# A hybrid convolution decoder block on one core: tiles of h and y moved by 160 bytes, other due times for h, norm and gate of mixer B, squares and taps shared by two engines, products taken from PSUM

## The chip, the core and the metric

The kernel runs on one core of a Trainium2 chip. Its engines are TensorE (PE; the loading of its stationary operand is shown apart as PEld), VectorE (DVE), ScalarE (ACT), GpSimd (POOL) and SyncE (SP, which issues nearly all DMAs here). The metric is the device time of one execution in microseconds; less is better. The kernel before takes 1806.1 us, the median of 3 runs (1805.6 to 1812.25).

## The reference

All arithmetic is float32; x is 256 tokens by 4096 channels. With D = 4096:

```
mod = silu(c) @ w_ada + b_ada            # 4096 -> 3 * 4096: shift, scale, gate
h   = rmsnorm(x, norm_g) * (1 + scale) + shift
P   = h @ w_in                           # 4096 -> 14336 columns: a_b a_c a_x a_z b_v b_g b_z, 2048 each
y_a = a_b * conv3(a_c * a_x) * silu(a_z)               # causal, depthwise
u   = conv31(b_v * sigmoid(b_g)) + conv_b_b            # causal, depthwise, 31 taps
y_b = silu(layernorm(u, ln_b_g, ln_b_b)) * silu(b_z)
x   = x + gate * (concat(y_a, y_b) @ w_out)            # 4096 -> 4096
out = rmsnorm(x, final_g)
```

## The kernel before

**Matrix products in three pieces.** A float32 weight tile `w_r` (128 channels x 2 x 512 columns, 512 KB) is split into a high half `w_h` (ScalarE, L215) and a low half `w_l` (VectorE, L216); h and y are split alike by `hi_part` (ScalarE, L248) and `lo_part` (VectorE, L251). `products` (L233) issues for each 128 channels k and each of the two token halves three matmuls: high x w_h (L242), high x w_l (L243), low x w_h (L244). The weights are the moving operand (512 columns), h or y the stationary one. One k of one column tile is a *unit*: 6 matmuls. A *step* is one weight tile, mostly two units (12 matmuls). w_in takes 28 column tiles x 32 k = 896 units, w_out 8 x 32 = 256: 1152 units, 6912 matmuls, 591 steps. The names w0 to w590 in the program count the steps.

**Blocks.** h needs shift and scale of its own channels, and these need 134 MB of w_ada, so w_in isn't walked column tile by column tile. `BLOCKS` cuts the 32 k into six blocks of 2, 4, 4, 6, 8 and 8; in each block all 28 column tiles are visited, partial sums being kept in `acc` tiles in SBUF and copied back to PSUM by `seed` (L593). At the start of a block its first column tile takes all new k one after the other, so pairs of new hT tiles (`hT24` holds k = 24, 25) are first used one step apart. In the last block `take` (L596) brings the finished sums out through ScalarE with the activation that the column tile wants (sigmoid for b_g, SiLU for a_z and b_z).

**What sets the order.** The program is recorded in the order in which Python runs, and each engine works through its instructions strictly in that order. `now` counts units. Every step first calls `next_w`, which records the load and the two splits of the weight tile two steps ahead:

```
        raw = raws.tile([P, KD, CT], F32, tag="r", name=f"w{i}_r")   # 4 buffers
        nc.sync.dma_start(raw[:, part], src[k // KD][:, part])
        ...                                                           # hi, lo: pool split, 3 buffers each
        nc.scalar.copy(hi[:, part], raw[:, part])
        nc.vector.tensor_tensor(out=lo[:, part], in0=raw[:, part], in1=hi[:, part].bitcast(F32), op=ALU.subtract)
```

then the pending `take`, then `seed` where the column tile ends, then `run_due`, which pops whatever `put(t, f)` has registered for t <= now, and then the step's matmuls. `w_h` of step s+2 uses the buffer that the matmuls of step s-1 read, so it waits for the end of step s-1. `run_due` also fills in the sums for shift, scale and gate (`ada_steps`, L261: a 1 MB row tile in one of 3 buffers, one VectorE pass of 2048 elements) where a model of VectorE's and the DMA's load leaves room or the sum falls due.

**h.** `h_steps` (L309) makes a pair of h tiles in five pieces: fetch (SP loads `xc` into a tile of pool `big`), by_token (VectorE), by_channel (two ScalarE instructions), high (ScalarE), low (VectorE). `H_LEAD` says how many units before its first use each is put; `H_DUE` how many before that use its sums fall due.

**Mixer A and B.** `silu_gate_A` (L411) multiplies the four accumulated tiles pairwise, transposes them by PE into `psA`, and applies the 3 taps. `glu_B` (L453) multiplies v by sigmoid(g), transposes into `psU`, keeps `uT`, and registers 30 taps (`conv_tap`, L490) for each of the four groups: four ScalarE multiplications into `pr` and one VectorE addition into `cv`. `norm_B` (L501) is the layer norm, `gate_B` (L567) transposes z into `psZ` (a pool of two PSUM buffers shared with the other transposes) and multiplies. y goes through `split_y`. The first half of w_out's k (y_A, sums `pa`) runs while mixer B ends; the second half (sums `pb`) follows.

**Where tiles lie.** Pools lie behind each other in SBUF. `split` (w_h, w_l) starts at byte 4096, `big` (acc, xc, hT, yT, pr, cv and others, 34 tiles of 4096 bytes) at byte 32096, which is 62 x 512 + 352. The last column tile of w_out keeps the first five of its eight weight steps (`HOLD = 5`) in tiles of `big` instead of `split`, works through token half 0, and then through token half 1.

Of the kernel before, what the change touches and what calls it, by code (L numbers as in the profile page):

```python
# [49 lines left out]

H_LEAD = (9, 6, 4, 2, 1)
H_DUE = 8
A_STEP = 3
CONV_END = 86
NORM_AT = 88
NORM_STEP = 2
# [15 lines left out]
def _segments():  # L72

    order = [16, 20, 17, 21, 18, 22, 19, 23]
    order += [e + i for i in range(4) for e in (4, 8, 0, 12)]
    order += [24, 25, 26, 27]
    segs, done = [], dict.fromkeys(order, 0)
    for b in range(len(BLOCKS)):
        for n, e in enumerate(order if (len(BLOCKS) - 1 - b) % 2 == 0 else order[::-1]):
            k0, k1 = done[e], sum(BLOCKS[:b + 1]) - (KD if n < EARLY.get(b, 0) else 0)  # L80
            if b == 0 and n < ALONE:
                k1 = 1
            done[e] = k1
# [24 lines left out]
def decoder_block(ctx: ExitStack, tc: tile.TileContext, x, c, w_mod, w_gate, w_in, w_out, xt, pk, final_g, out):  # L108
# [237 lines left out]
    sums = const.tile([P, NS, 8], F32, name="sums")  # L346
    table(AF.Silu)
    for q in range(4):
        ps = pst(f"cps{q}")
        for h in range(2):  # L350
            nc.tensor.matmul(ps[:, h], ones[:1], crow[q][:1, h * CT:(h + 1) * CT], start=True, stop=True)
        nc.scalar.activation(out=cB[:, q * 1024:(q + 1) * 1024], in_=ps, func=AF.Silu)
        for i in ((), (0, 1), (2, 3, 4), (5, 6, 7))[q]:
            nc.scalar.activation(out=xn[i], in_=xn[i], func=AF.Square, accum_out=sums[:, i % 2, i // 2:i // 2 + 1])
    table(AF.Sqrt)
# [21 lines left out]
    first_h[1][0]()  # L377
    first_mod[2]()
    next_w()
    first_mod[3]()  # L380
    for f, _ in first_h[2:]:
# [29 lines left out]
    def silu_gate_A(i):  # L411

        p, xa, q, z = (acc[e] for e in (4 + i, 8 + i, i, 12 + i))
        tiles, pss = {}, {}

        def gates():
            nc.vector.tensor_tensor(out=p, in0=p, in1=xa, op=ALU.mult)
            nc.vector.tensor_tensor(out=q, in0=q, in1=z, op=ALU.mult)

# [22 lines left out]
        t = now + 2  # L442
        put(t, gates, 2.3)
        for j in range(4):
            t += A_STEP
            put(t, lambda j=j: turn(j))
            put(t + 0.1, lambda j=j: tap(j))
            put(t + 2, lambda j=j: rest(j), 1.15)

# [3 lines left out]
    def glu_B(i):  # L453
        nonlocal conv_start
        v, g = acc[16 + i], acc[20 + i]
        pss = {}

        def gated():
            nc.vector.tensor_tensor(out=v, in0=v, in1=g, op=ALU.mult)

# [16 lines left out]

        put(now + 2, gated, 1.15)
        for h in range(2):
            put(now + 5, lambda h=h: turn(h))  # L480
            put(now + 5.1 + h, lambda h=h: keep(h))
        put(now + 8, tap)
        conv_start = conv_start or now + 10
        w = (conv_end - conv_start) / 4
        for sh in range(1, TAPS):
            t = max(now + 10, conv_start + i * w)
            t += (sh - 1) * (conv_start + (i + 1) * w - t) / (TAPS - 1)
            put(t, lambda sh=sh, t=t: conv_tap(i, sh, t))
# [107 lines left out]
    def take(e, k1, ps):  # L596

        if e not in acc:
            acc[e] = bigt(f"acc{e}")
        func = AF.Copy  # L600
        if k1 == KT:
            func = AF.Sigmoid if 20 <= e < 24 else AF.Silu if e >= 24 or 12 <= e < 16 else AF.Copy
        nc.scalar.activation(out=acc[e], in_=ps, func=func)  # L603
# [200 lines left out]
```

## Time and profile before

| | |
|---|---|
| median of 3 runs | 1806.1 us |
| the profiled execution | 1817.72 us, of it 1815.9 us from the first to the last instruction |
| PE busy | 1702.5 us, 94% |
| VectorE, ScalarE busy | 1383.5 us (76%), 1171.3 us (64%) |
| mean granted clock of PE | 0.972 |
| DMA | 524 MB through SP's queue, mean 290 GB/s |

The profiled execution is the one whose rows are shown below; its stages are cut at the first matmul of weight steps 0, 96, 368, 464, 512 and 544 and at the last matmul, that is at 0, 162, 706, 898, 994, 1058 and 1152 units. Matmuls are pipelined, so that a matmul's duration is longer than the distance between two starts; the distance is what counts.

### The profile page before, as it was taken

The numbers are of one execution on the slowest core, as the hardware profiler recorded it, in microseconds if no ns is written. First come the engines' busy times: TensorE is split into PE (matmuls) and PEld (weight loads), VectorE is DVE, ScalarE is ACT, GpSimd is POOL, SyncE is SP. The second block draws the span as 40 slices with busy tenths as digits, with TensorE's granted clock in tenths as the row PEclk, the third lists the DMA queues.
The fourth block names the chain that finished last, engine by engine and source line by source line (L and its number), as shares of the span: only waits on it lengthen the run. The fifth ranks groups of instructions, "written<-read, shape, count | busy, mean of one in ns | idle before, by whom it ended". The sixth has DMA issues, their size and how long they took to land. (4 is left out here: it accounts for less than half of the span.)

```text
span 1815.9 us, 20052 instructions
## 1 busy us (share of the span) xinstructions
PE 1702.5 (94%) x7069; PEld 1347.3 (74%) x7069; DVE 1383.5 (76%) x1329; ACT 1171.3 (64%) x1587; POOL 1.0 (0%) x8
## 2 busy tenths in 40 slices
PE   5989989999799998899999979999999999969997
PEld 2767868888688886688888857777777888748885
DVE  4877867888688887688888858888888977736556
ACT  5776657655465555455555548999999887534444
POOL 0000000000000000000000000000000000000000
PEclk9999989999899999899999989999999999979998
DMA  8998989999799999699999977666565766537775
GB/s 311 387 351 302 346 310 349 373 375 381 264 364 377 371 379 346 249 361 375 380 370 378 353 261 282 220 222 196 172 196 188 264 188 187 172 105 231 233 233 184
DMA packets 122284, 526.02 MB, mean 290 GB/s; under 512 B 13476, under 2 KB 13764, under 8 KB 97608
## 3 DMA queue, kind: packets, MB, share of 16 engines
q1 hardware_dynamic: 121992, 524.36, 80.4%
q8 instruction: 56, 0.92, 0.2%
q10 hardware_dynamic: 192, 0.39, 0.1%
q14 instruction: 44, 0.36, 0.1%
HBM read 520.48 MB, written 4.21 MB: 289 GB/s over the span
## 5 line engine op out<-in xcount | busy, mean ns | idle before, releaser
L216 DVE TENSOR_TENSOR w_l<-w_r,w_h 128x1024 fp32r<-128x1024 f32 (+1 forms) x591 | 705.5, 1196 | 388.1 <-ACT w_h L215 387.1
L215 ACT CAST w_h<-w_r 128x1024 fp32r<-128x1024 f32 (+1 forms) x591 | 606.0, 1026 | 599.1 <-PE ps L244 428.1
L244 PE MATMUL ps<-w_h,hT 128*128 128x512 f32 x1792 | 724.9, 405 | 43.3 <-DVE hT L251 43.3
L242 PE MATMUL ps<-w_h,hT 128*128 128x512 f32 x1792 | 725.8, 405 | 19.9 <-ACT hT L248 11.6
L243 PE MATMUL ps<-w_l,hT 128*128 128x512 f32 x1792 | 721.2, 402 | 0.5 <-DVE w_l L216 0.3
L244 PEld LDWEIGHTS ps<-w_h,hT 128*128 128x128 f32 x1792 | 345.2, 193 | 134.0 <-DVE hT L251 50.6
L242 PEld LDWEIGHTS ps<-w_h,hT 128*128 128x128 f32 x1792 | 345.5, 193 | 111.1 <-ACT hT L248 13.5
L243 PEld LDWEIGHTS ps<-w_l,hT 128*128 128x128 f32 x1792 | 344.8, 192 | 84.5 <-DVE w_l L216 1.8
L494 ACT ACTIVATE pr<-uT,pks 128x255 f32<-128x255 f32 (+14 forms) x480 | 198.6, 487 | 0.6 <-DVE cv L497 0.5
L603 ACT ACTIVATE acc<-ps 128x1024 f32<-128x1024 f32 x163 | 166.3, 1021 | 0.0
L269 DVE CUSTOM_DVE_ANT_0 mod<-mod,cB,pts 128x2048 f32<-128x2048 f32 x64 | 150.2, 2347 | 1.9 <-DMA mod<-in_w_mod 1.9
L269 DVE CUSTOM_DVE_ANT_0 mod<-mod,cB,pks 128x2048 f32<-128x2048 f32 x64 | 150.2, 2346 | 0.7 <-DMA mod<-in_w_mod 0.7
L497 DVE TENSOR_TENSOR cv<-cv,pr 128x1020 f32<-128x1020 f32 (+14 forms) x120 | 138.5, 1154 | 0.0
L593 ACT COPY ps<-acc 128x1024 f32<-128x1024 f32 x135 | 136.4, 1010 | 0.0
L242 PE MATMUL pb<-w_h,yT 128*128 128x512 f32 x256 | 104.3, 407 | 0.0
L243 PE MATMUL pb<-w_l,yT 128*128 128x512 f32 x256 | 103.6, 405 | 0.0
L244 PE MATMUL pb<-w_h,yT 128*128 128x512 f32 x256 | 103.4, 404 | 0.0
L242 PE MATMUL pa<-w_h,yT 128*128 128x512 f32 x256 | 102.6, 401 | 0.0
L243 PE MATMUL pa<-w_l,yT 128*128 128x512 f32 x256 | 101.9, 398 | 0.0
L244 PE MATMUL pa<-w_h,yT 128*128 128x512 f32 x256 | 101.9, 398 | 0.0
L269 DVE CUSTOM_DVE_ANT_0 gate<-gate,cB,pts 128x2048 f32<-128x2048 f32 x32 | 75.1, 2346 | 0.0
L269 DVE CUSTOM_DVE_ANT_0 gate<-gate,cB,pks 128x2048 f32<-128x2048 f32 x32 | 75.1, 2346 | 0.0
(111 smaller groups left out, 655.3 us busy)
## 6 DMA issues: line engine op xcount, KB each, us to landing
w_r<-in_w_in SPq DMA_DIRECT2D x433, 512.0 KB, 5.5
mod<-in_w_mod SPq DMA_DIRECT2D x128, 1024.0 KB, 7.7
gate<-in_w_gate SPq DMA_DIRECT2D x64, 1024.0 KB, 7.5
w_r<-in_w_out SPq DMA_DIRECT2D x128, 512.0 KB, 4.1
w_r<-in_w_in SPq DMA_DIRECT2D x30, 256.0 KB, 3.9
xn<-in_x SPq DMA_DIRECT2D x8, 512.0 KB, 6.3
xr<-in_x SPq DMA_DIRECT2D x8, 512.0 KB, 6.4
out<-o SPq DMA_DIRECT2D x16, 256.0 KB, 2.5
```

Source lines behind the costliest of these rows:

```text
L215: nc.scalar.copy(hi[:, part], raw[:, part])
L216: nc.vector.tensor_tensor(out=lo[:, part], in0=raw[:, part], in1=hi[:, part].bitcast(F32), op=ALU.subtract)
L242: nc.tensor.matmul(out, ah, hi[:, i], start=f, stop=False, skip_group_check=seeded)
L243: nc.tensor.matmul(out, ah, lo[:, i], start=False, stop=False, skip_group_check=seeded)
L244: nc.tensor.matmul(out, al, hi[:, i], start=False, stop=l, skip_group_check=seeded)
L269: nc.vector.tensor_tensor_reduce(out=raw, in0=raw, in1=cB[:, q * ROW:(q + 1) * ROW], scale=1.0, scalar=pt if q else bias, op0=ALU.mult, op ...
L494: nc.scalar.activation(out=pr[:, j, sh:], in_=u[:, j, :S - sh], func=AF.Copy, scale=cbw[:, 4 * i + j, TAPS - 1 - sh:TAPS - sh])
L497: nc.vector.tensor_tensor(out=o[:, :, sh:], in0=o[:, :, sh:], in1=pr[:, :, sh:], op=ALU.add)
L593: nc.scalar.copy(ps, acc[e])
L603: nc.scalar.activation(out=acc[e], in_=ps, func=func)
```

## The change

Seven groups of edits:

- A tile of 40 floats (160 bytes) is added to pool `const`, so that `big` starts at byte 32256 = 63 x 512; `split` stays at 4096.
- `H_LEAD` and `H_DUE` put every piece of h earlier, `low` 3 units instead of 1 before the first use.
- The column order is changed so that g comes before v, and a_b last of its four; `take` then multiplies the second factor straight out of PSUM on VectorE, in place of a ScalarE copy and a later VectorE product.
- Steps of mixer A are 4 units apart instead of 3, its first transposes come 2 units after the last sum instead of 5; those of `glu_B` 2 and 4 units after instead of 5.
- Every third tap of the 31-tap convolution is four VectorE instructions (multiply and add) and none on ScalarE.
- The taps end, and the norm starts, 12 units earlier; the gate of mixer B takes 4 units per group instead of 2.
- At the start four of the eight sums of squares go to VectorE, and the fourth sum for channel 0 precedes the first weight tiles.

```
+FILL = 40
-H_LEAD = (9, 6, 4, 2, 1)
-H_DUE = 8
-A_STEP = 3
-CONV_END = 86
-NORM_AT = 88
+H_LEAD = (15, 9, 7, 5, 3)
+H_DUE = 10
+A_STEP = 4
+CONV_END = 74
+NORM_AT = 76
...
-    order = [16, 20, 17, 21, 18, 22, 19, 23]
-    order += [e + i for i in range(4) for e in (4, 8, 0, 12)]
+    order = [20, 16, 21, 17, 22, 18, 23, 19]
+    order += [e + i for i in range(4) for e in (4, 8, 12, 0)]
...
+    const.tile([P, FILL], F32, name="fill")
...
+        if i % 2 == 0:
+            nc.scalar.activation(out=xn[i], in_=xn[i], func=AF.Square, accum_out=total)
+        else:
+            nc.vector.tensor_tensor_reduce(out=xn[i], in0=xn[i], in1=xn[i], ..., accum_out=total)
...
-        for i in ((), (0, 1), (2, 3, 4), (5, 6, 7))[q]:
+        for i in ((1, 2, 3), (4, 5), (6, 7), ())[q]:
...
+    first_mod[3]()
     next_w()
-    first_mod[3]()
...
-        put(t, gates, 2.3)
         for j in range(4):
-            t += A_STEP
-            put(t, lambda j=j: turn(j))
+            put(t + A_STEP * j, lambda j=j: turn(j))
...
-        put(now + 2, gated, 1.15)
         for h in range(2):
-            put(now + 5, lambda h=h: turn(h))
+            put(now + 2 + 2 * h, lambda h=h: turn(h))
...
     def conv_tap(i, sh, at):
         u, o = uT[i], cv[i]
+        if sh % 3 == 0:
+            for j in range(4):
+                nc.vector.scalar_tensor_tensor(out=o[:, j, sh:], in0=u[:, j, :S - sh], scalar=cbw[...], in1=o[:, j, sh:], op0=ALU.mult, op1=ALU.add)
+            return
...
+        other = {8: (e - 4, e - 4), 0: (e + 12, e), 16: (e + 4, e)}.get(e // 4 * 4)
+        if k1 == KT and other:
+            a, dst = (acc[j] for j in other)
+            nc.vector.tensor_tensor(out=dst, in0=ps, in1=a, op=ALU.mult)
...
-            t = end_in + NORM_AT + NORM_STEP * (18 + i + 0.5 * h)
+            t = end_in + NORM_AT + NORM_STEP * (18 + 2 * i + h)
...
-        put(t + 2.5, hi)
-        put(t + 3.5, lo, 0.65)
+        put(t + 2, hi)
+        put(t + 4, lo, 0.65)
```

VectorE's instructions around the first use of hT24 and hT26, at the start of the last block. PE reads hT24 in the step of w351, hT26 in that of w352. Before:

```order
L216 TENSOR_TENSOR w351_l_7347<-w351_r_7344,w351_h_7346 128x1024
L319 TENSOR_TENSOR xc26_7329<-xc26_7329,rstd_171 128x512
L269 ISA gate21_0_7355,pts_102<-gate21_0_7355,cB_103,pks_60 128x2048
L269 ISA pts_102 128x1
L216 TENSOR_TENSOR w352_l_7373<-w352_r_7370,w352_h_7372 128x1024
L319 TENSOR_TENSOR xc28_7350<-xc28_7350,rstd_171 128x512
L216 TENSOR_TENSOR w353_l_7398<-w353_r_7395,w353_h_7397 128x1024
L251 TENSOR_TENSOR hT24_7378<-xc24_7306,hT24_7378 128x2x256
```

After, in the same place:

```order
L218 TENSOR_TENSOR w351_l_7355<-w351_r_7352,w351_h_7354 128x1024
L321 TENSOR_TENSOR xc28_7292<-xc28_7292,rstd_172 128x512
L271 ISA gate21_0_7363,pts_103<-gate21_0_7363,cB_104,pks_60 128x2048
L271 ISA pts_103 128x1
L218 TENSOR_TENSOR w352_l_7381<-w352_r_7378,w352_h_7380 128x1024
L253 TENSOR_TENSOR hT24_7358<-xc24_7247,hT24_7358 128x2x256
L321 TENSOR_TENSOR xc30_7314<-xc30_7314,rstd_172 128x512
L218 TENSOR_TENSOR w353_l_7405<-w353_r_7402,w353_h_7404 128x1024
L253 TENSOR_TENSOR hT26_7385<-xc26_7267,hT26_7385 128x2x256
```

The low half of hT24 stood behind the split of w353 and stands now behind that of w352, one step earlier; a sum for gate (L271) stands ahead of that split.

SP's DMA issues at the same block start. xc28 goes into the tile that hT16 held, which PE reads last in the step of w347; xc30 into that of hT18, read last in the step of w348. Before:

```order
L210 DMA w350_r_7323<-in_w_in 128x1024
L316 DMA xc26_7329<-in_xt 128x512
L210 DMA w351_r_7344<-in_w_in 128x1024
L316 DMA xc28_7350<-in_xt 128x512
L268 DMA gate21_0_7355<-in_w_gate 128x2048
L210 DMA w352_r_7370<-in_w_in 128x1024
L316 DMA xc30_7376<-in_xt 128x512
L210 DMA w353_r_7395<-in_w_in 128x1024
```

After:

```order
L318 DMA xc26_7267<-in_xt 128x512
L270 DMA gate20_0_7269<-in_w_gate 128x2048
L212 DMA w348_r_7284<-in_w_in 128x1024
L318 DMA xc28_7292<-in_xt 128x512
L212 DMA w349_r_7306<-in_w_in 128x1024
L318 DMA xc30_7314<-in_xt 128x512
L270 DMA gate20_1_7316<-in_w_gate 128x2048
L212 DMA w350_r_7331<-in_w_in 128x1024
```

xc28, which waits for PE to end its work on hT16 (step of w347), stood ahead of the load of w352 and stands now ahead of that of w349; xc30 now ahead of that of w350.

VectorE's instructions for the gate of mixer B, its first three groups (`psZ1_0` is group 1, half 0). Before:

```order
L578 TENSOR_TENSOR cv0_7673<-cv0_7673,psZ0_0_11750 128x512
L216 TENSOR_TENSOR w529_l_11804<-w529_r_11801,w529_h_11803 128x1024
L578 TENSOR_TENSOR cv0_7673<-cv0_7673,psZ0_1_11777 128x512
L251 TENSOR_TENSOR yT8_11783<-cv0_7673,yT8_11783 128x2x256
L578 TENSOR_TENSOR cv1_7884<-cv1_7884,psZ1_0_11784 128x512
L216 TENSOR_TENSOR w530_l_11847<-w530_r_11844,w530_h_11846 128x1024
```

After:

```order
L584 TENSOR_TENSOR cv0_7651<-cv0_7651,psZ0_0_11549 128x512
L218 TENSOR_TENSOR w523_l_11599<-w523_r_11596,w523_h_11598 128x1024
L584 TENSOR_TENSOR cv0_7651<-cv0_7651,psZ0_1_11578 128x512
L253 TENSOR_TENSOR yT8_11577<-cv0_7651,yT8_11577 128x2x256
L218 TENSOR_TENSOR w524_l_11632<-w524_r_11629,w524_h_11631 128x1024
L584 TENSOR_TENSOR cv1_7865<-cv1_7865,psZ1_0_11608 128x512
```

Two half groups per step became one, and the whole has moved six steps ahead (w529 to w523).

## Rows read from the trace of the kernel before

**Rows 1.** Stages: us; PE, PEld, DVE, ACT, POOL busy; PE clock; DMA share, GB/s.
```profile
36.40:294.20 257.80, 241.89 (x972) 187.69 (x973) 196.45 (x196) 175.27 (x200) 0.00 (x0) 0.97 0.89 335
294.20:1113.60 819.40, 786.50 (x3273) 628.24 (x3272) 645.77 (x586) 456.46 (x481) 0.00 (x0) 0.97 0.93 349
1113.60:1413.40 299.80, 286.12 (x1242) 227.06 (x1241) 261.90 (x267) 284.36 (x514) 0.00 (x0) 0.99 0.63 204
1413.40:1549.70 136.30, 136.01 (x582) 109.14 (x581) 110.28 (x97) 111.34 (x201) 0.00 (x0) 1.00 0.68 211
1549.70:1671.30 121.60, 104.81 (x422) 83.13 (x421) 68.36 (x69) 58.84 (x75) 0.00 (x0) 0.90 0.52 163
1671.30:1802.90 131.60, 131.60 (x565) 106.00 (x563) 82.58 (x80) 62.38 (x81) 0.00 (x0) 1.00 0.68 222
```
**Rows 2.** The same view, of short stretches in which PE never waits.
```profile
80.00:100.00 20.00, 20.00 (x87) 16.10 (x86) 18.70 (x18) 13.37 (x16) 0.00 (x0) 1.00 1.02 414
440.00:460.00 20.00, 20.00 (x87) 16.09 (x86) 17.24 (x17) 13.45 (x16) 0.00 (x0) 1.00 1.02 406
900.00:1000.00 100.00, 100.00 (x428) 80.42 (x427) 82.22 (x71) 53.15 (x54) 0.00 (x0) 1.00 1.00 375
```
**Rows 3.** Timeline of PE, last token half: start, duration (us), engine, line, tiles, operands.
```profile
1793.39 0.39 PE L242 MATMUL pb<-w_h,yT 128*128 128x512 f32 x1
...
1798.83 0.40 PE L242 MATMUL pb<-w_h,yT 128*128 128x512 f32 x1
...
1799.53 0.39 PE L242 MATMUL pb<-w_h,yT 128*128 128x512 f32 x1
...
1802.34 0.40 PE L242 MATMUL pb<-w_h,yT 128*128 128x512 f32 x1
```
**Rows 4.** Waits (us, times, longest): stage one; stage two; whole span.
```profile
PE ps L244 <- DVE hT L251: 10.5, 5, 3.1
...
PE ps L244 <- DVE hT L251: 32.9, 11, 4.8
...
PE psZ L575 <- DVE cv L578: 16.5, 5, 3.7
```
**Rows 5.** Timeline of all engines at one start of a block (idle time before, releaser).
```profile
1055.68 1.04 ACT L215 CAST w_h<-w_r 128x1024 fp32r<-128x1024 f32 x1 [4.53 <-PE ps L244]
...
1056.76 1.23 DVE L216 TENSOR_TENSOR w_l<-w_r,w_h 128x1024 fp32r<-128x1024 f32 x1 [2.38 <-ACT w_h L215]
...
1057.90 0.69 DVE L251 TENSOR_TENSOR hT<-xc,hT 128x512 fp32r<-128x512 f32 x1
...
1058.64 0.79 PE L244 MATMUL ps<-w_h,hT 128*128 128x512 f32 x1 [2.52 <-DVE hT L251]
```
**Rows 6.** DMA issues: tile, queue, count, KB each, median us from issue to landing.
```profile
w_r<-in_w_out SPq DMA_DIRECT2D x128, 512.0 KB, 4.1
```
**Rows 7.** Timeline of all engines, start of the program.
```profile
3.18 13.99 PE L351 MATMUL cps<-crow,ones 1*128 1x512 f32 x16 [3.18 <-DMA crow<-in_c]
...
21.98 0.16 DVE L361 TENSOR_REDUCE tiny<-sums 128x2 f32<-128x8 f32 x1 [21.98 <-ACT xn L354]
...
31.13 1.89 DVE L216 TENSOR_TENSOR w_l<-w_r,w_h 128x512 fp32r<-128x512 f32 x3
...
32.93 2.35 DVE L269 CUSTOM_DVE_ANT_0 mod<-mod,cB,pts 128x2048 f32<-128x2048 f32 x1
...
36.41 0.79 PE L242 MATMUL ps<-w_h,hT 128*128 128x512 f32 x1 [9.20 <-ACT hT L248]
```
**Rows 8.** Groups by line: count, busy us, mean ns of one, idle before.
```profile
L494 ACT ACTIVATE pr<-uT,pks 128x255 f32<-128x255 f32 (+14 forms) x480 | 198.6, 487 | 0.6 <-DVE cv L497 0.5
L497 DVE TENSOR_TENSOR cv<-cv,pr 128x1020 f32<-128x1020 f32 (+14 forms) x120 | 138.5, 1154 | 0.0
L435 DVE SCALAR_TENSOR_TENSOR yfA<-psA,pks,yfA 128x255 f32<-128x255 f32 (+1 forms) x32 | 15.3, 480 | 0.9 <-ACT yfA L430 0.3
L673 DVE TENSOR_TENSOR o<-pb,gate 128x1024 f32<-128x1024 f32 x7 | 8.5, 1218 | 0.0
```

More of the change, by code (lines that the diff above doesn't have):

```diff
@@ L347, in decoder_block, with row_squares @@
     table(AF.Silu)
+    def row_squares(i):
+        total = sums[:, i % 2, i // 2:i // 2 + 1]
+        if i % 2 == 0:
+            nc.scalar.activation(out=xn[i], in_=xn[i], func=AF.Square, accum_out=total)
+        else:
+            nc.vector.tensor_tensor_reduce(out=xn[i], in0=xn[i], in1=xn[i], scale=1.0, scalar=0.0, op0=ALU.mult, op1=ALU.add, accum_out=total)
+    row_squares(0)
     for q in range(4):
@@ L352, in decoder_block @@
         nc.scalar.activation(out=cB[:, q * 1024:(q + 1) * 1024], in_=ps, func=AF.Silu)
-        for i in ((), (0, 1), (2, 3, 4), (5, 6, 7))[q]:
-            nc.scalar.activation(out=xn[i], in_=xn[i], func=AF.Square, accum_out=sums[:, i % 2, i // 2:i // 2 + 1])
+        for i in ((1, 2, 3), (4, 5), (6, 7), ())[q]:
+            row_squares(i)
     table(AF.Sqrt)
@@ L411, in silu_gate_A @@
     def silu_gate_A(i):
-        p, xa, q, z = (acc[e] for e in (4 + i, 8 + i, i, 12 + i))
+        p, q = acc[4 + i], acc[i]
         tiles, pss = {}, {}
-        def gates():
-            nc.vector.tensor_tensor(out=p, in0=p, in1=xa, op=ALU.mult)
-            nc.vector.tensor_tensor(out=q, in0=q, in1=z, op=ALU.mult)
         def turn(j):
@@ L442, in silu_gate_A @@
         t = now + 2
-        put(t, gates, 2.3)
         for j in range(4):
-            t += A_STEP
-            put(t, lambda j=j: turn(j))
-            put(t + 0.1, lambda j=j: tap(j))
-            put(t + 2, lambda j=j: rest(j), 1.15)
+            put(t + A_STEP * j, lambda j=j: turn(j))
+            put(t + A_STEP * j + 0.1, lambda j=j: tap(j))
+            put(t + A_STEP * j + 2, lambda j=j: rest(j), 1.15)
     uT, cv, zB = {}, {}, {}
@@ L454, in glu_B @@
         nonlocal conv_start
-        v, g = acc[16 + i], acc[20 + i]
+        v = acc[16 + i]
         pss = {}
-        def gated():
-            nc.vector.tensor_tensor(out=v, in0=v, in1=g, op=ALU.mult)
         def turn(h):
@@ L599, in take @@
             acc[e] = bigt(f"acc{e}")
[L600 to L603, printed above, removed]
+        other = {8: (e - 4, e - 4), 0: (e + 12, e), 16: (e + 4, e)}.get(e // 4 * 4)
+        if k1 == KT and other:
+            a, dst = (acc[j] for j in other)
+            nc.vector.tensor_tensor(out=dst, in0=ps, in1=a, op=ALU.mult)
+        else:
+            func = AF.Copy
+            if k1 == KT:
+                func = AF.Sigmoid if 20 <= e < 24 else AF.Silu if e >= 24 or 12 <= e < 16 else AF.Copy
+            nc.scalar.activation(out=acc[e], in_=ps, func=func)
         if k1 < KT:
             return
-        if 20 <= e < 24:
-            glu_B(e - 20)
+        if 16 <= e < 20:
+            glu_B(e - 16)
         elif e >= 24:
             zB[e - 24] = acc[e]
-        elif 12 <= e < 16:
-            silu_gate_A(e - 12)
+        elif e < 4:
+            silu_gate_A(e)
     def begin_step():
```

11 lines of the change are left out of this document (6 added, 5 removed).

## The prediction

> **What bounds the kernel now.** I read the table of stages first [rows 1]. PE is busy in 242 of 258 us, 786 of 819, 286 of 300, 136 of 136, 105 of 122 and 132 of 132, so PE is what the time is made of. How far is it from its own pace? Where it never waits it starts 428 matmuls in 100 us [rows 2], 233.6 ns each and 1.402 us per unit of 6. The six stages hold 162, 544, 192, 96, 64 and 94 units, which at this pace take 227.1, 762.7, 269.2, 134.6, 89.7 and 131.8 us; the stages lose 30.7, 56.7, 30.6, 1.7, 31.9 and 0 us over that. Before the first matmul lie 36.4 us [rows 7], after the last one 13.0. So 1,615 us are matmuls at pace, 152 us losses, 49 us ends.
>
> Then the waits [rows 4]: PE waited for the low half of hT 10.5 us in the first stage and 32.9 us in the second, and 16.5 us for the gate of mixer B. The rest of the losses in those stages is clock: a mean of 0.97 over 819 us means some 6% of it at the lower level (1.2 GHz), which costs half of that time, 25 us; 0.90 over 122 us costs 12 us. Each drop follows a wait. In the stage of 300 us there is little of either: ScalarE is busy in 284 of it, so there ScalarE is as much the bound as PE.
>
> **1. The 160 bytes.** Nearly all matmuls read weights at multiples of 4096 and hT or yT 352 bytes past a multiple of 512. The last column tile has both kinds side by side: five kept weight steps lie in the same pool as yT, three don't. In token half 1, 24 starts over kept tiles lie in 1793.39 to 1798.83, 226.7 ns each; 12 over the others in 1799.53 to 1802.34, 234.2 ns each [rows 3]. Same clock, same yT pool, no waits. I read this as: a matmul runs 6.8 ns faster where both operands start at the same place within 512 bytes (the kept tiles are all over the pool, so it is not one address). After the change all of them do. Per unit that is 41 ns, 1.402 to 1.361 us. I take it in full where PE sets its own pace: 544 units 22.2 us, 96 units 3.9, 64 units 2.6, 94 less the 10 kept ones 3.4; half of 6.6 us in the first stage, where DMA is at 414 GB/s [rows 2] and can't follow a faster PE; nothing in the 300 us stage (see 4). Sum 35.4. Can DMA follow elsewhere? At 375 GB/s and 1.402 us per unit [rows 2] it moves 0.526 MB per unit; at 1.361 us that is 386 GB/s, and 406 were reached with PE at full pace. Bounds: no gain at all if something other than the place within 512 bytes makes the difference; from below nothing excludes a loss, since no pair that starts at multiples of 512 on both sides is in the trace.
> A rule of the Trainium skill speaks against this edit: SBUF — State Buffer, section Door 1, says that SBUF is read in lines of 16 bytes and only crossing to a new line costs. Both 0 and 352 are line starts, so by it the edit is worth nothing and the sum would be 1716. The trace's 226.7 against 234.2 ns does not agree with it; it is the first rival.
>
> **2. h earlier.** What ends last at a block start is a chain [rows 5]: PE ends a step, w_h starts (1055.68), w_l follows (1056.76), and the low half of hT stands behind it (1057.90 to 1058.59): 2.9 us from release to end. It was recorded in the very step that needs it, so PE stops for 2.52 us, at each pair, and the clock falls. Recorded one step earlier, the same chain has 12 matmuls and the two that don't need the low half, 14 x 226.7 ns = 3.17 us: it fits, by 0.26 us. What is late next: in each of the last three block starts one sum of 2.35 us stands between (first excerpt): VectorE then is about 1.3 us late once or twice, 5 us in all. And the fetches, also earlier, now stand ahead of urgent weights (second excerpt): SP waits at xc28 until PE has left hT16, and queued behind it is w349, needed one step later. Issue to landing 4.1 us [rows 6], w_h 1.04 and w_l 1.14 make 6.3 us, less the 2.72 us step and one matmul: 3.3 us of stall; 2 more at w350; another 3.3 at the start two blocks' lengths before (xc22 before w238). Slow clock after these: some 4 us. So of the 56.7 us I leave 18 and take 38.7. In the first stage the low-half waits make 10.5 us; with a little of the clock I take 12.7 of the 30.7 lost, and leave 18 for slow first matmuls, late DMA and the earlier due times. Together 51.4; bounds 35 (every earlier piece late by a sum) and 70.
>
> **3. The start.** ScalarE's eight squares hold up the reduction until 21.98 [rows 7]. With four on VectorE, ScalarE is through when the last broadcast of c is (PE ends it at 17.2), and the root comes about 3.7 us earlier. The fourth sum (32.93) stood behind three weight splits (31.13, together 1.89 us); these now come after it, and only 0.63 us of them is in the way of the second matmul. 5.5 us; bounds 0 (its row tile lands late) and 6.
>
> **4. Mixer stage, 300 us.** 28 of some 84 taps in it move. Each takes four ScalarE instructions off (487 ns, 1.6 us overlapped) and one addition off VectorE (1.15), and puts four multiply-adds on it [rows 8]. The trace has these only from PSUM, in pairs that wait on each other: 480 ns. I bound one between 0.40 us (overlapping the next by 0.09, as w_l of 1.23 us is followed after 1.14 us in rows 5) and 0.515 (the 480 ns and a gap to the next, if each waits for the one before). So ScalarE goes from 284 to about 226 us, 12 copies of about 1 us gone too (w_h, as long, takes 1.04 in rows 5), and VectorE from 262 [rows 1] to between 275 and 288; I take 281. The products cost VectorE the same from PSUM as from SBUF (1218 ns for 1024 columns [rows 8]). PE itself needs 192 x 1.361 = 261 plus about 10 of transposes. So VectorE becomes the bound. Before, the stage took 5% over its busiest engine; I give VectorE 10 us for that: 291, a gain of 9; bounds 276 and 304.
>
> **5. Norm and gate of B.** Two half groups of psZ per step with two buffers made PE wait for VectorE's product, which stood behind a w_l that itself waited for PE: 16.5 us [rows 4] and 12 us of clock. Now one half group is done per step (third excerpt), and its product ends 2.9 us after a step's end by the chain of rows 5, as the buffer is wanted 2.72 us plus the transposes later: no wait. Transposes stay (31.9 - 16.5 - 12 = 3.4 us for 8 groups), and I leave 4 for the chain of the norm. Gain 24.4; bounds 10 and 28. The taps' earlier end costs nothing by itself: the stage behind has VectorE busy in 110 of 136 us.
>
> **Sum.** 35.4 + 51.4 + 5.5 + 9 + 24.4 = 125.7 us off the profiled span of 1815.9, giving 1690.2. The profiled execution took 1817.72 us (1.8 outside the span), 11.6 above the median of the runs; the runs differ in their stalls, and taking the same 125.7 off the median 1806.1 gives 1680.4. I forecast 1680.
>
> **Rivals.**
> - *The alignment does nothing*: 1680 + 35.4 = 1716. For it: kept and other tiles differ also in pool, and the two pools now agree within 512 but not within 1024 bytes. Against it: kept tiles at quite different addresses all run alike.
> - *It does more*: kept tiles and yT both lie 32 bytes past a multiple of 64, which may itself cost what the mismatch costs, 6.8 ns. Without it 219.9 ns, another 35 us: 1645. DMA would need 398 GB/s, under the 406 seen. The Trainium skill (TensorE: Matmul & The Clock Gate, back-to-back issue gap) gives about 216 ns for 512 columns at full clock; no row here comes near it, and by it the sum would be some 20 us lower still.
> - *VectorE is a harder bound than I think*: multiply-adds at 0.515 us, and its lag delays w_l in the stage behind too. 304 for 291, and 12 us more: 1705. For it: VectorE would be at 95% and works strictly in order.
> - *Slower than before*: the opposite of 1. If operands that both start at multiples of 512 bytes get in each other's way, every matmul pays: 6.9 us per ns. The other terms give 90 us, so it decides from 13 ns on, an interval of 247 ns; at 250 the time is 1829. For it: no row has such a pair. Against it: the kept pair agrees within 512 bytes too and is the faster one.
>
> **How the numbers follow.** Chances: forecast 0.62 (its own range 1655 to 1705), alignment nothing 0.20, more 0.10, VectorE 0.04, slower 0.04. The range that leaves out no more than 2 in 10 runs from 1640, which takes in the third case, to 1722, which takes in the first rival with some bad luck in 2 and 4. A difference of under 0.5%, 9 us, is what a measurement of this kernel can't tell from none. All cases but the last are faster by far more: faster 0.95, same 0.01, slower 0.04.
>
> **What would show it.** Step 1: starts 226.7 ns apart, some 441 matmuls per 100 us where PE doesn't wait; 428 would mean that the first rival holds. Step 2: the wait of PE for hT under 10 us instead of 43.4, clock at 0.99; new ScalarE waits for w_r's DMA of about 3 us at w238 and w349. Step 3: first matmul at 31 instead of 36.4. Step 4: VectorE over 95% busy in the mixer stage, w_h no longer waiting for ScalarE's taps. Step 5: no wait of psZ over 1 us. The forecast is wrong above all if the matmul interval is another, or if the new place of the fetches stalls PE for more than 10 us in all.

## The result, and the profile after

The changed kernel takes 1732.7 us, the median of 4 runs (1730.1 to 1740.1), against 1808.2 us (4 runs, 1805.6 to 1812.3): a ratio of 0.959 (0.955 to 0.963). It is faster by 4.1%, as its sign was forecast, but by 75 us where 126 were forecast, and the time lies above the range. The profiled execution took 1730.07 us with a span of 1728.3.

The stages of the changed kernel, cut at the same weight steps as [rows 1], with the same columns (the last window ends 1.1 us after the last matmul has started; the table behind it goes from start to start):

```profile
31.50:271.60 240.10, 230.26 (x972) 182.95 (x973) 197.63 (x198) 175.66 (x201) 0.00 (x0) 0.99 0.96 362
271.60:1043.60 772.00, 751.18 (x3276) 616.46 (x3275) 648.86 (x592) 459.11 (x487) 0.00 (x0) 0.99 0.96 372
1043.60:1348.20 304.60, 282.79 (x1239) 226.53 (x1238) 275.92 (x351) 233.79 (x393) 0.00 (x0) 0.98 0.62 199
1348.20:1480.20 132.00, 131.62 (x581) 108.75 (x580) 116.63 (x133) 92.37 (x145) 0.00 (x0) 1.00 0.68 216
1480.20:1587.80 107.60, 96.51 (x423) 77.70 (x422) 61.83 (x64) 55.31 (x72) 0.00 (x0) 0.97 0.60 187
1587.80:1716.60 128.80, 128.07 (x566) 105.70 (x564) 83.25 (x81) 62.53 (x81) 0.00 (x0) 1.00 0.70 229
```

Laid against the forecast stage by stage (the forecast is the length before, less the terms that the prediction gives to the stage):

| stage (units) | before | forecast | after | missed by |
|---|---|---|---|---|
| up to the first matmul | 36.4 | 30.9 | 31.6 | 0.7 |
| first (162) | 257.8 | 241.8 | 240.1 | -1.8 |
| second (544) | 819.4 | 758.5 | 772.0 | 13.5 |
| mixer (192) | 299.7 | 290.7 | 304.5 | 13.8 |
| w_out, y_A (96) | 136.3 | 132.4 | 132.1 | -0.3 |
| gate of B (64) | 121.6 | 94.6 | 107.6 | 13.0 |
| last (94) | 131.5 | 128.1 | 127.6 | -0.5 |

So three stages miss by 13 to 14 us each, and all else came out. The remaining 14 us of the miss are no stage's: the prediction took its 125.7 us off the median of three runs, which lay 11.6 us below the profiled execution that the terms were read from, and the profiled execution after lies 2.7 us below its own median.

The density of matmuls where PE never waits, against the last row of [rows 2]:

```profile
850.00:950.00 100.00, 100.00 (x443) 82.81 (x442) 85.48 (x73) 55.52 (x55) 0.00 (x0) 1.00 1.00 387
```

443 starts in 100 us instead of 428, and DMA follows with 387 GB/s (386 were worked out). The waits of the whole span, against [rows 4]:

```profile
ACT w_h L217 <- DMA w_r<-in_w_in: 48.8, 27, 7.9
...
ACT yT L250 <- DVE yfA L444: 17.0, 8, 3.4
...
PE ps L246 <- DVE hT L253: 10.7, 8, 3.3
...
PE psU L468 <- DVE acc L610: 9.5, 4, 3.4
...
PE psZ L581 <- DVE cv L584: 6.9, 2, 3.8
...
PE psA L433 <- DVE acc L610: 6.6, 4, 1.9
...
PE pb L244 <- ACT pb L728: 3.4, 1, 3.4
```

The wait for hT fell from 43.4 to 10.7 us and that for psZ from 16.5 to 6.9. In their place stand a wait of up to 7.9 us for a weight's DMA, waits for the products (`acc`) before the transposes psU and psA, one of ScalarE for yfA, and one for the seed of pb. Each was followed to its place.

**Second stage.** The timeline of SP, ScalarE and PE at the start of the last block:

```profile
956.71 0.33 SPq L212 DMA_DIRECT2D w_r<-in_w_in  x1
969.99 0.33 SPq L318 DMA_DIRECT2D xc<-in_xt  x1
970.41 0.38 SPq L212 DMA_DIRECT2D w_r<-in_w_in  x1
972.71 0.33 SPq L318 DMA_DIRECT2D xc<-in_xt  x1
973.09 0.42 SPq L270 DMA_DIRECT2D gate<-in_w_gate  x1
973.61 0.85 SPq L212 DMA_DIRECT2D w_r<-in_w_in  x2
...
974.43 1.04 ACT L217 CAST w_h<-w_r 128x1024 fp32r<-128x1024 f32 x1 [7.90 <-DMA w_r<-in_w_in]
...
975.53 0.50 PE L244 MATMUL ps<-w_h,hT 128*128 128x512 f32 x1 [2.85 <-ACT w_h L217]
...
977.38 0.63 PE L246 MATMUL ps<-w_h,hT 128*128 128x512 f32 x1
977.81 0.63 PE L244 MATMUL ps<-w_h,hT 128*128 128x512 f32 x1
...
988.40 0.50 PE L246 MATMUL ps<-w_h,hT 128*128 128x512 f32 x1 [3.26 <-DVE hT L253]
```

SP issued w348 at 956.71 and then stood for 13 us at xc28, until PE had left the tile of hT16. The weight behind it was issued at 970.41; its w_h starts 4 us later, and PE has waited for it. So far this is the stall that was forecast (3.3 us; PE shows 2.85). What was not: the standing used up the whole lead of the loads. Seven transfers, two of them of 1 MB (the second gate tile goes out at 974.51), then start within 5 us, w_h waits for its weight twice more (3.09 and 0.38 us), VectorE's low half of hT comes 3.26 us late at 988.40, and after the first stall the matmuls start 0.43 us apart for 2.6 us (977.38, 977.81). That is the lower clock level, 1.2 GHz: the granted clock between 976.5 and 980.3 is 0.55.

**Mixer stage.** VectorE is busy for 275.9 of 304.6 us, 91% where over 95% were forecast, and less than the 281 us forecast: the multiply-adds came out at the low end of the bounds (112 of them cover 44.9 us, 0.40 each). It idles for 28.7 us, 25.5 of it before w_l, waiting for ScalarE's w_h. Timeline of VectorE and PE up to the longest of the new waits for a product; it lies at the end of the second stage, just ahead of the cut at 1043.6:

```profile
1031.22 1.23 DVE L218 TENSOR_TENSOR w_l<-w_r,w_h 128x1024 fp32r<-128x1024 f32 x1 [2.22 <-ACT w_h L217]
...
1033.49 2.35 DVE L271 CUSTOM_DVE_ANT_0 gate<-gate,cB,pts 128x2048 f32<-128x2048 f32 x1
...
1035.76 2.36 DVE L218 TENSOR_TENSOR w_l<-w_r,w_h 128x1024 fp32r<-128x1024 f32 x2
...
1039.28 1.66 DVE L496 SCALAR_TENSOR_TENSOR cv<-uT,pks,cv 128x253 f32<-128x253 f32 x4
1040.86 1.22 DVE L218 TENSOR_TENSOR w_l<-w_r,w_h 128x1024 fp32r<-128x1024 f32 x1
1041.99 1.22 DVE L610 TENSOR_TENSOR acc<-ps,acc 128x1024 f32<-128x1024 f32 x1
...
1043.27 0.66 PE L468 MATMUL psU<-ident,acc 128*128 128x128 f32 x4 [3.43 <-DVE acc L610]
```

Starved until 1031.22, VectorE then works without a pause, and the product that PE's transposes need is at the end of that row of work. It was queued only one step before PE asks for it, and PE stands for 3.43 us. In the mixer stage itself PE waits 11.1 us for such products; before the change it was 7.9. What grew most there is ScalarE's wait for yfA: 17.0 us, all in this stage, against this line of the stage before the change:

```profile
ACT yT L248 <- DVE yfA L436: 1.3, 2, 0.6
```

**Gate of B.** The tile gate_ps (the sums of gate, transposed by PE for the store to DRAM) comes from the same pool of two buffers as psZ. Its writer and reader, by tile:

```profile
L300 PE MATMUL gate_ps<-ident,gateT x1: 270/270/270, 1501.1 to 1501.1; 128*32 128x128 f32 x1
L303 ACT COPY gate_row<-gate_ps x1: 238/238/238, 1516.3 to 1516.3; 32x128 f32<-32x128 f32 x1
```

and the timeline of that stretch:

```profile
1507.53 0.68 DVE L584 TENSOR_TENSOR cv<-cv,psZ 128x512 f32<-128x512 f32 x1
...
1508.36 0.63 PE L581 MATMUL psZ<-ident,acc 128*128 128x128 f32 x4 [3.80 <-DVE cv L584]
...
1515.59 0.68 DVE L584 TENSOR_TENSOR cv<-cv,psZ 128x512 f32<-128x512 f32 x1
...
1516.30 0.24 ACT L303 COPY gate_row<-gate_ps 32x128 f32<-32x128 f32 x1
...
1516.41 1.09 PE L581 MATMUL psZ<-ident,acc 128*128 128x128 f32 x4 [3.08 <-DVE cv L584]
```

gate_ps holds its buffer from 1501.1 to 1516.3. The two waits for psZ fall into just that time, where one buffer was left.

### The profile page after: what moved, and what is told of

Its sections match the earlier page's. It is cut to its first block, busy times and chain, and to the rows that moved or that the text cites. A ratio compares the mean times of both kernels' runs of the same rounds, so it can differ in the third digit from the quotient of the medians.

```text
span 1728.3 us, 19974 instructions
## 1 busy us (share of the span) xinstructions
PE 1635.6 (95%) x7069; PEld 1324.2 (77%) x7069; DVE 1406.6 (81%) x1457; ACT 1097.8 (64%) x1407; POOL 1.0 (0%) x8
## 4 chain that ended last, share of the span: by engine, by line
PE 73%; DVE 9%; ACT 7%; DMA 5%; issue 5%; SPq 0%; DVEq 0%; ACTq 0%
PE ps L244 18%; PE ps L246 18%; PE ps L245 18%; DVE w_l L218 3%; PE pb L244 3%; PE pb L246 3%; PE pb L245 3%; DMA w_r<-in_w_in 3%; PE pa L245 3%; PE pa L246 3%; PE pa L244 3%; ACT w_h L217 3%; DMA mod<-in_w_mod 2%; ACT pr L500 1%; DVE cv L503 1%
## 5 line engine op out<-in xcount | busy, mean ns | idle before, releaser
L244 PE MATMUL ps<-w_h,hT 128*128 128x512 f32 x1792 | 708.5, 395 | 22.9 <-ACT hT L250 8.8
L245 PE MATMUL ps<-w_l,hT 128*128 128x512 f32 x1792 | 705.1, 393 | 11.3 <-DVE w_l L218 11.3
L246 PE MATMUL ps<-w_h,hT 128*128 128x512 f32 x1792 | 704.3, 393 | 10.8 <-DVE hT L253 10.7
L244 PEld LDWEIGHTS ps<-w_h,hT 128*128 128x128 f32 x1792 | 339.6, 190 | 103.0 <-ACT ps L599 12.7
L245 PEld LDWEIGHTS ps<-w_l,hT 128*128 128x128 f32 x1792 | 339.9, 190 | 88.1 <-DVE w_l L218 19.0
L246 PEld LDWEIGHTS ps<-w_h,hT 128*128 128x128 f32 x1792 | 339.3, 189 | 86.7 <-DVE hT L253 15.6
L615 ACT ACTIVATE acc<-ps 128x1024 f32<-128x1024 f32 x151 | 153.9, 1019 | 0.0
L271 DVE CUSTOM_DVE_ANT_0 mod<-mod,cB,pks 128x2048 f32<-128x2048 f32 x64 | 150.2, 2346 | 4.1 <-DMA mod<-in_w_mod 4.0
L271 DVE CUSTOM_DVE_ANT_0 mod<-mod,cB,pts 128x2048 f32<-128x2048 f32 x64 | 150.1, 2346 | 2.1 <-DMA mod<-in_w_mod 2.1
L500 ACT ACTIVATE pr<-uT,pks 128x255 f32<-128x255 f32 (+19 forms) x320 | 132.4, 487 | 0.0
L244 PE MATMUL pb<-w_h,yT 128*128 128x512 f32 x256 | 99.7, 390 | 3.4 <-ACT pb L728 3.4
L246 PE MATMUL pb<-w_h,yT 128*128 128x512 f32 x256 | 99.6, 389 | 0.0
L245 PE MATMUL pb<-w_l,yT 128*128 128x512 f32 x256 | 99.6, 389 | 0.0
L503 DVE TENSOR_TENSOR cv<-cv,pr 128x1020 f32<-128x1020 f32 (+9 forms) x80 | 92.4, 1155 | 0.0
L271 DVE CUSTOM_DVE_ANT_0 gate<-gate,cB,pts 128x2048 f32<-128x2048 f32 x32 | 75.0, 2345 | 0.9 <-DMA gate<-in_w_gate 0.9
L271 DVE CUSTOM_DVE_ANT_0 gate<-gate,cB,pks 128x2048 f32<-128x2048 f32 x32 | 75.0, 2345 | 0.0
```

The source lines that it names most:

```text
L244: nc.tensor.matmul(out, ah, hi[:, i], start=f, stop=False, skip_group_check=seeded)
L245: nc.tensor.matmul(out, ah, lo[:, i], start=False, stop=False, skip_group_check=seeded)
L246: nc.tensor.matmul(out, al, hi[:, i], start=False, stop=l, skip_group_check=seeded)
L271: nc.vector.tensor_tensor_reduce(out=raw, in0=raw, in1=cB[:, q * ROW:(q + 1) * ROW], scale=1.0, scalar=pt if q else bias, op0=ALU.mult, op ...
```

## The experiments

In all of them the kernel before ran on the same chip; its medians there were 1810.7, 1811.8 and 1814.5 us (7 runs each), up to 6 us above the 1808.2 of the result. The changed kernel was not run again beside them, so a difference of a few us between totals says little; stages that an edit doesn't touch agree within 1 us in the mixer stage and 4 us in the second. Stage lengths are those of the profiled execution.

**1. The places by themselves.** A kernel that only multiplies: 48 matmuls for each of 18 pairs of places.

```
PLACES = [(0, 0), (0, 352), (352, 352), (352, 0), (0, 16), (0, 32), (0, 64), (0, 128), (0, 256), (0, 384),
          (32, 32), (16, 16), (32, 0), (64, 64), (64, 0), (32, 352), (0, 352), (0, 0)]
nc.tensor.matmul(ps, sta[:, b:b + P], mov[:, a:a + 512], ...)   # a, b: the place, plus a multiple of 4096 bytes
```

> This kernel computes nothing of the block: on one core without DMA traffic it runs 48 float32r matmuls (128x128 by 512 columns) for each of 18 pairs of places, the moving operand m and the stationary operand s bytes past a multiple of 512. Theory (same place within 512 bytes): about 226.7 ns per matmul for (0,0), (352,352), (32,32), (16,16) and (64,64), about 233.6 ns for every other pair. Rival 1 (only the place within 64 bytes counts): 226.7 ns also for (0,64), (0,128), (0,256), (0,384), (64,0) and (32,352), and 233.6 ns only where the difference is no multiple of 64: (0,16), (0,32), (32,0), (0,352), (352,0). Rival 2 (the place does not matter, the kept tiles were faster for another reason): one and the same interval for all pairs.

Timeline of PE: start, duration of the whole group, tile (qa is the first pair, qb the second, and so on):

```profile
59.50 11.04 PE L45 MATMUL qa<-mov,sta 128*128 128x512 f32 x48
70.38 11.41 PE L45 MATMUL qb<-mov,sta 128*128 128x512 f32 x48
81.62 11.07 PE L45 MATMUL qc<-mov,sta 128*128 128x512 f32 x48
92.53 11.37 PE L45 MATMUL qd<-mov,sta 128*128 128x512 f32 x48
...
148.50 11.10 PE L45 MATMUL qi<-mov,sta 128*128 128x512 f32 x48
159.43 11.32 PE L45 MATMUL qj<-mov,sta 128*128 128x512 f32 x48
170.58 11.09 PE L45 MATMUL qk<-mov,sta 128*128 128x512 f32 x48
181.51 11.26 PE L45 MATMUL ql<-mov,sta 128*128 128x512 f32 x48
192.61 11.37 PE L45 MATMUL qm<-mov,sta 128*128 128x512 f32 x48
```

From one group's start to the next, over 48: (0,0) 226.7 ns, (0,352) 234.2, (352,352) 227.3. The new pair and the old one differ as in the kernel, with no load under way and no other engine reading the two operands, so it is the place itself. The theory's rule is nearly right: of the five pairs that agree within 512 bytes four take 226.7 to 227.7 and (16,16) takes 231.3; but (0,256), which agrees only within 256 bytes, is as fast at 227.7. Of the others (64,0) takes 229.0 and all the rest 232.3 to 234.2, multiples of 64 among them. Both rivals fall.

**2. Without the 160 bytes.**

```
-    const.tile([P, FILL], F32, name="fill")
```

> The changed kernel without the 160 bytes, everything else as changed. Theory (the place of h and y against the weights makes 6.9 ns per matmul): starts 233.6 ns apart where PE runs freely, 544 units of the second stage cost 22 us more (772 to 794), and 4, 3 and 3 us more in the three stages of w_out; total 1760 to 1770 us. In the mixer stage nothing, if VectorE and ScalarE set its pace (304 us as now); 4 to 8 us more there if PE's own pace still counts. Rival (something else in the change made the matmuls denser): 226.7 ns and 1730 us as with the 160 bytes.

1774.2 us (ratio 0.978, 0.975 to 0.982), 41 more than the changed kernel. The same view as above:

```profile
850.00:950.00 100.00, 100.00 (x428) 80.42 (x427) 82.86 (x72) 53.59 (x54) 0.00 (x0) 1.00 0.99 374
```

428 again. The stages cost 3.7, 26.4, 2.7, 4.3, 4.5 and 3.9 us more. The theory holds, though the total lies 4 us above the 1760 to 1770 expected. By the medians the term is 41 us where 35.4 were forecast; some of the difference can be run and chip. The second stage takes more of it than the forecast gave (26.4 for 22.2); that slower matmuls make the stalls around them dearer may be the reason, but no run shows it.

**3. The fetch of x two steps later, still in SP's queue.**

```
-H_LEAD = (15, 9, 7, 5, 3)
+H_LEAD = (11, 9, 7, 5, 3)
```

> The changed kernel with the fetch of x at 11 units ahead (in whole steps: 10) in place of 15, all other leads as changed. Theory (SP's queue stands for 13 us at xc22 and at xc28 until PE leaves the old tile, and the weights behind it come late): the two waits of ScalarE for w_r (9.4 us around 660, 11.4 us around 972) go to under 1 us, the stretches around the two block starts lose under 4 us each instead of 11 and 19, the second stage takes 750 to 760 us instead of 772, total 1712 to 1720 us. Rival (VectorE's sums and the passes by token are what is late there): the fetches being later, by_token waits for them and the low halves of hT come later still; second stage 768 us or more, total 1726 us or more.

1727.7 us, second stage 767.3: neither the theory's time nor quite the rival's. SP still stood for 7.5 and 4.6 us before two fetches at the last block start, the loads lost their lead as before, and the low half of hT came 6.7 us late. The trial was too small a step: at both leads the old tile isn't free yet when SP comes to the fetch, and SP stands.

**4. The fetch of x in GpSimd's queue, lead as changed.**

```
-            nc.sync.dma_start(st["x"], xt[:, ks[0]:ks[0] + n])
+            (nc.gpsimd if ks[0] else nc.sync).dma_start(st["x"], xt[:, ks[0]:ks[0] + n])
```

> The changed kernel with the fetches of x on GpSimd's queue in place of SP's (all but the first), lead 15 as changed: the fetch still waits for PE to leave the old tile, but no weight stands behind it. Theory (the standing queue of SP is what costs at the two block starts): no wait of ScalarE for w_r over 1 us around 660 and 972, the two stretches of 32 steps take 90 and 92 to 94 us (now 97.8 and 106.6), second stage 750 to 756 us in place of 772, total 1708 to 1716 us. Rival (the block start asks more of the DMA or of VectorE than it can give, whatever the queue): second stage 764 us or more, the low halves of hT late by 3 us or more at the same places.

1716.1 us (ratio 0.946, 0.943 to 0.949). The second stage:

```profile
271.90:1029.20 757.30, 744.37 (x3277) 613.16 (x3277) 648.95 (x592) 459.33 (x487) 4.30 (x8) 1.00 0.99 378
```

757.3 us in place of 772.0, 1 us above what was expected; the stretches of 32 steps around the block starts take 90.8 and 98.8 us (92 to 94 were expected of the latter; 4.9 of it are the waits for psU), and no w_h waits for a weight there. The fetch waits just as long, but on an engine with nothing behind it. This is the cause of the second stage's miss: 14.7 us for the queue that stood. The Trainium skill (DMA: Bandwidth & Descriptors, Issuing engines are not separate DMA queues) says that issuing from several engines saves only the sequencer's time to start a transfer, usually little. Here the 8 fetches of this stage, moved, are worth 14.7 us, because what the sequencer of SP spent was the wait ahead of the transfer.

**5. The leads of h as before the change.**

```
-H_LEAD = (15, 9, 7, 5, 3)
-H_DUE = 10
+H_LEAD = (9, 6, 4, 2, 1)
+H_DUE = 8
```

> The changed kernel with the leads and due times of h as before the change (9, 6, 4, 2, 1 and 8), everything else as changed. It says what the earlier h alone is worth, of which the prediction took 12.7 us in the first stage and 38.7 in the second. Theory (SP's standing queue gave back some 14 us of the 38.7): first stage 250 to 254 us in place of 240, second stage 795 to 802 us in place of 772, total 1764 to 1772 us. Rival (the earlier h brought its full 38.7 us, and another part of the change lost 13 us in the second stage): second stage 808 to 813 us, total 1778 us or more.

1774.8 us, first stage 256.2, second 799.4, PE's wait for hT 41.6 us in all. The second stage is where the theory put it (795 to 802); the first stage and the total lie 2 to 3 us above their ranges, the total still under the rival's 1778. The earlier h brings 16.2 us in the first stage (forecast 12.7) and 27.3 in the second; with experiment 4 it is 42.1 there (38.7 were forecast).

**6. The transposes one step later.**

```
-        t = now + 2
+        t = now + 4                                    # psA, its taps and products
...
-            put(now + 2 + 2 * h, lambda h=h: turn(h))
+            put(now + 4 + 2 * h, lambda h=h: turn(h))  # psU; first taps 2 units later too
```

> The changed kernel with the first transposes of mixer A and of u, and all that follows them, one step later (4 units after the sum in place of 2). Theory (the products are asked for one step after they were queued on VectorE, whose queue is several us behind): the waits for acc before psU (9.5 us) and psA (6.6 us) go to under 3 us in all; the mixer stage takes 290 to 296 us in place of 304.6, the second stage 4 us less, total 1714 to 1720 us. Rival (VectorE has too much work in the stage, and PE waits for it one way or the other): the waits for acc turn into waits for w_l, mixer stage 300 to 306 us, total 1726 us or more.

1717.0 us, mixer stage 292.3, second stage 767.3. The waits for acc in the mixer stage fell from 11.1 to 0.6 us, and what showed next was ScalarE: 19.6 us before the high halves of y, PE waiting 11.5 us for seeds behind them:

```profile
ACT yT L250 <- DVE yfA L444: 19.6, 8, 4.5
```

**7. The split of y_A one step later as well.**

```
-                put(now + 2, hi)
-                put(now + 4, lo, 0.65)
+                put(now + 4, hi)
+                put(now + 6, lo, 0.65)
```

> As the kernel with the transposes one step later, and the high and low halves of y of mixer A one step later too. Theory (ScalarE stands for 17.0 us before the high halves of y until VectorE has multiplied yfA, and w_h and then w_l behind it): ScalarE's wait for yfA goes under 4 us, PE's waits for w_l from 6.9 to under 3 us, mixer stage 5 to 8 us shorter than with the transposes alone. Rival (ScalarE's standing costs nothing, since VectorE is late anyway): the stage within 2 us of that with the transposes alone.

1707.3 us (ratio 0.942, 0.940 to 0.945). The mixer stage, and two of its waits:

```profile
1038.50:1323.70 285.20, 277.16 (x1241) 223.46 (x1240) 279.18 (x359) 239.42 (x402) 0.00 (x0) 1.00 0.66 215
```

```profile
DVE w_l L218 <- ACT w_h L217: 3.9, 7, 1.3
...
ACT yT L250 <- DVE yfA L444: 0.5, 1, 0.5
```

VectorE does the same work as after the change (279 and 276 us), but in 285 us instead of 304.5: its idle time fell from 28.7 to 6, and the granted clock of the stage rose from 0.98 to 1.00. PE's waits for w_l stayed at 6.0 us (under 3 were expected); the 7 us came from the seeds, for which PE now waits 1.4 instead of 11.5.

**8. All taps on ScalarE.** `conv_tap` without its branch for every third tap.

> The changed kernel with all 30 taps as before the change: four multiplications on ScalarE and one addition on VectorE each. By the rows of the changed kernel this takes about 28 x (4 x 0.39 - 1.15) = 12 us off VectorE in the mixer stage (276 to 264) and puts 28 x 1.65 = 46 us on ScalarE (234 to 280). Theory (due times, not VectorE's work, make the results late): mixer stage 300 to 308 us, the waits for acc within 4 us of the 11 us now. Rival (VectorE's work makes them late): waits for acc halved, mixer stage 288 to 296 us.

1738.8 us; the mixer stage:

```profile
1049.90:1357.50 307.60, 283.67 (x1239) 227.59 (x1238) 266.93 (x272) 276.99 (x509) 0.00 (x0) 0.98 0.63 207
```

With 9 us less to do, VectorE still makes PE wait 15.1 us for acc. So its work isn't what made these products late. The other wait, that of ScalarE for yfA, did go, at the same due time (17.0 us after the change):

```profile
ACT yT L250 <- DVE yfA L444: 2.2, 5, 0.6
```

So that one does come from the work that VectorE was given; the later due time of experiment 7 makes room for it. The length of the stage can't tell the two apart, since 43 us of work went to ScalarE. Sharing the taps was worth 3 us where the due times were short.

**9. The gate's sums and their transpose 8 units earlier.**

```
-    gates_due = end_in + KT // 2 * NDT - 20
+    gates_due = end_in + KT // 2 * NDT - 28
```

> The changed kernel with the gate's sums due, and its transpose into PSUM with them, 8 units earlier. Theory (the transpose gate_ps holds one of the two psZ buffers from 1510 to 1516 us, just as the gate groups of mixer B start, 12 units earlier than before the change): the two waits for psZ (3.8 and 3.1 us) go, and with them the slow clock behind them; the stage of 64 units takes 96 to 100 us instead of 107.6, the wait of 3.4 us for the seed of pb stays; total 1719 to 1723 us. Rival (the product of a group comes late behind w_l, and that behind w_h and the SiLUs of the norm, whatever holds the other buffer): both waits stay, stage 105 to 108 us, total 1728 to 1733 us.

1725.6 us (ratio 0.953, 0.950 to 0.955), somewhat above the time expected; the stage takes 100.5 us instead of 107.6, and the waits for psZ go from 6.9 to 0.7 us. gate_ps was the cause.

**10. The four together,** with the seed of pb0 recorded one step before its use.

```
+            if dt == NDT - 1 and k + KD == KT // 2:
+                first_b = seed_b(0)
             run_due()
...
-                ps = seed_b(0)
+                ps = first_b
```

> The changed kernel with the four causes mended together: fetches of x on GpSimd's queue, transposes and splits of mixer A and u one step later, the gate's sums and its transpose 8 units earlier, and the seed of pb0 one step before its use. If the causes are separate and their gains add: first matmul at 31.5, stages of 240, 752, 285, 132, 97 and 128 us, tail 13 and 1.8 outside the span, 1676 to 1684 us. Rival (the gains overlap, as a mended wait only shows the next): 1690 us or more, the mixer stage above 290.

1677.1 us (ratio 0.924, 0.922 to 0.927), 56 us below the changed kernel. The second, the mixer and the gate's stage:

```profile
274.20:1023.80 749.60, 742.86 (x3273) 612.88 (x3273) 643.98 (x585) 455.25 (x478) 4.30 (x8) 1.00 0.99 381
1023.80:1309.00 285.20, 277.09 (x1241) 223.45 (x1241) 279.16 (x359) 239.38 (x402) 0.00 (x0) 1.00 0.65 214
...
1441.00:1536.30 95.30, 93.48 (x423) 75.57 (x422) 61.83 (x64) 55.13 (x72) 0.00 (x0) 1.00 0.67 212
```

The single gains were 16.7 (experiment 4), 25.4 (7) and 7.1 us (9), together 49.2; the seed of pb0 was not tried alone, and the gate's stage is 5.3 us shorter than in 9. With these they add up to 54.5 of the 55.7 us. The clock's mean is 0.998.

**11. The same with every fifth tap on VectorE.**

```
-        if sh % 3 == 0:
+        if sh % 5 == 0:
```

> As the kernel with the four causes mended, with every fifth tap on VectorE in place of every third: some 12 taps of the mixer stage go back to ScalarE. Theory (with the due times mended VectorE's work is the bound, 279 of 285 us): VectorE has 5 us less to do there, ScalarE 20 us more (239 to 259), and the stage takes 278 to 282 us; total 4 to 6 us less than with every third tap. Rival (the stage is held by the order of the queues, not by VectorE's work): stage within 2 us of the one with every third tap, total the same.

1679.0 us (ratio 0.926, 0.924 to 0.928): not faster. The mixer stage is 288.2 us, with VectorE at 276.0 and ScalarE at 256.4. The theory falls. Of the rival the total comes out; its stage is 3.0 us longer, where it should have been within 2. What keeps the stage at 285 is open: PE is busy for 277 of it and VectorE for 279, and 3 us less on VectorE bring nothing.

## Why the prediction was right in sign and wrong in size

**The 160 bytes: right.** 226.7 ns, 443 starts per 100 us, DMA at 387 GB/s; 35.4 us were forecast, 41 measured. The last token half of the kernel before, with both kinds of places side by side [rows 3], was enough to read the interval to 0.1 ns. The rule of the Trainium skill that the prediction set against it (SBUF — State Buffer, Door 1) says that an access that crosses to a new 16-byte line costs. It says nothing of where two operands start against each other, so whoever goes by it alone leaves the 41 us out. The prediction's reading of the 6.8 ns was too narrow in one point: agreement within 256 bytes does as well as within 512.

**The first stage and the start: right.** 240.1 us for 241.8, first matmul at 31.6 for 30.9.

**h in the second stage: the mechanism right, a cost too small.** "3.3 us of stall; 2 more at w350; another 3.3" priced the one weight behind the fetch: issue to landing, w_h, w_l, less the step. 18 us of loss were left in the stage, and 32.2 came (772.0 less 544 units at 1.360 us). The term should have counted for how long SP stands: 13 us there are nearly five steps of loads, and whoever comes after pays as well. With the fetches out of SP's queue (experiment 4) 17.5 us are left in the stage, close to the 18 of the sum, so this queue is the step that failed; the prediction had itself named a stall of over 10 us at the new place of the fetches as a sign of being wrong. 4.9 us of the 32.2 are psU's waits from the last column tiles of this stage, the next point.

**The mixer stage: the term that failed most.** "Before, the stage took 5% over its busiest engine; I give VectorE 10 us for that: 291". VectorE's work was forecast well (281; 276 measured), the idle time was not (10; 28.7 measured). "The products cost VectorE the same from PSUM as from SBUF" is true of their duration, but the edit also asks for the product one step after it is queued, where before it was two. And VectorE's new work makes yfA late, for whose high half the due time was left as it was, so that ScalarE stands before it and w_h behind it. The chain that the prediction had itself priced for hT at 2.9 us against a step of 2.72 (w_h, w_l, then the piece that is wanted) stands here again, with a product of 1.22 us at its end and whatever VectorE is behind with. By experiments 6 and 7 these two due times cost 19.3 us, some of it clock; with them mended the stage takes 285 us, below the 291.

The rival that VectorE is a harder bound named this stage and even its length, 304 us, but not the reason: VectorE did less than forecast and idled more, and the stage behind, for which the rival wanted 12 us, came out at 132.1.

**The gate of B: a user of the pool forgotten.** "no wait" counted psZ alone in its two buffers. The norm and the gate moved 12 units earlier, the gate's store did not, and so the two met: 7.1 us with the clock. The seed of pb0 behind the last high half of y was the other part, 3.4 us of wait; with both mended the stage takes 95.2 us against 94.6 forecast.

**The base.** Taking the gain off the median of three runs, 11.6 us under the profiled execution, assumed that the changed kernel's median would lie as far below its profiled execution. That execution was the fastest of its four runs instead, 2.7 us below the median.

Against 1680 us forecast stand 1732.7, and 1677.1 with four due times or queues mended: what the forecast priced was there to be had, and what it left out was what each moved piece meets in its new place. That 1677.1 comes so near to 1680 is partly luck: of the profiled executions 1678.6 stands against 1692.0 by the sum, the second stage having come out 9 us and the mixer stage 5 us below their terms.

## What to carry to other kernels

Where an edit hands a result to another engine, price the queue that the result stands in, not only its duration: how many instructions lie between its recording and its use, and what the producer does in that time. Where a transfer that waits for a buffer is moved earlier, it takes everything behind it in its queue along; put it in a queue of its own. When one user of a shared pool moves, list all the others, and look for the one that didn't move.

## What the runs showed of the hardware

- In one run over 16 different pairs of places, float32r matmuls whose moving and stationary operand start at the same place within 256 bytes took 226.7 to 227.7 ns per 512 columns, others 232.3 to 234.2; exceptions are (16,16) with 231.3 and (64,0) with 229.0, while (0,64) took 233.3 (the moving operand's place first). At 64 bytes the order of the two mattered, for a reason that stays open.
- 226.7 ns was the lowest mean interval of any stretch in these runs, also with nothing else running on the core. The Trainium skill (TensorE: Matmul & The Clock Gate, Back-to-back issue gap) gives about 216 ns for 512 columns at full clock as the gap of a single matmul, and 131 ns as the sustained one; no run here came to either.
- A fetch of 256 KB in GpSimd's queue landed 6.1 us after its issue (experiment 4, median of 15) against 6.5 in SP's after the change, and the issuing took 0.54 us of an engine that had no other work after the first 2 us.
